# Feed-forward first layers on TensorE: one 512-column product over both parts of h, halves added afterwards, and the PSUM pools exchanged

## The chip, the cores and the metric

The kernel runs on one core of one Trainium2 chip. The metric is the device time of one execution in microseconds (us). Lower is better. The engines are called PE (TensorE, matrix products; PEld is its weight load), DVE (VectorE), ACT (ScalarE), POOL (GpSimd) and SP (SyncE, whose queue issues most of the transfers).

## The reference

Two transformer blocks over 256 tokens with 1024 features, in float32. The first holds a stick-breaking attention and a mixture of 32 experts and isn't touched by the change in what it computes. The second is cut here to what matters:

```python
def swiglu(x, w_in, w_out):
    gate, up = jnp.split(x @ w_in, 2, axis=-1)
    return (jax.nn.silu(gate) * up) @ w_out

x = x + 0.5 * swiglu(rmsnorm(x, ffn1_norm_g), ffn1_w_in, ffn1_w_out)
...
x = x + mixer(rmsnorm(x, mix_norm_g))
x = x + 0.5 * swiglu(rmsnorm(x, ffn2_norm_g), ffn2_w_in, ffn2_w_out)
x = rmsnorm(x, final_norm_g)
```

The hidden width of a feed-forward is 2816. The mixer runs an mLSTM branch and a gated unit (SGU) beside it, multiplies both by sigmoid gates, adds them and sends the sum through an output matrix.

## The kernel before, in words

**Numbers in two parts.** In the second block every float32 value that goes to PE is split into a rounded part r and a remainder l, and a product is taken as wr·hr + wr·hl + wl·hr. Weights are split as they arrive: `split_w` (L162) lets ACT copy 128x1024 values into r (L167) and DVE subtract to get l (L169). There are three buffers for each part, so a split waits until the matmuls of the third split before it are through.

**The feed-forward.** `ffn` (L774) is called twice: first layer and output of the first feed-forward carry the prefix fa, of the second fb. The hidden width is worked in NF = 22 tiles of 128. For tile j, `inner(j)` takes the product of the gate half and of the up half (i = 0, 1) with the whole h, over KT = 8 slices of 128 features, 256 tokens wide: `mm_feat` issues three matmuls of 256 columns for every slice. Both halves go into one PSUM bank, tile `gu`. `gated(j)` multiplies the bank by the normalisation factors `rb` (DVE, L787, from PSUM into SBUF), takes silu on ACT (L789), multiplies (L790) and splits the result into pr (L793) and pl (L794). `outer(j)` adds the tile's share of the second layer into accumulators in PSUM: for fa 8 blocks of 256 columns with three matmuls each, for fb 4 blocks of 512 columns. Up to three `inner` products run ahead of `gated` and `outer`. Names in the profile drop numbers at the end: `fagu` stands for all fagu0 to fagu21, `fawi20r` keeps its own.

**Head of a feed-forward.** The normalisation factor isn't known when the first products start. The squares of x are summed into rows, two matmul groups of one column (`fas` in fa, `fbs` in fb) sum them over the features, a chain of small DVE operations makes the inverse square root, and `spread` multiplies diagonal tiles with ones into `fab`/`fbb` and copies that to `rb` (L183). Only then can `gated(0)` run. The dictionary `between` puts these steps behind certain `inner` calls (1 and 2.5), and in fb it puts transposes of x (`tokens`, tiles x5t, copied by ACT, L1185) behind inner 5 to 8.

**The mixer.** Its projections are made by `tok_half`, 48 matmuls of 512 columns into one two-bank tile each (mv, mo, mg, ms and others). `gate` reads such a tile with a sigmoid on ACT (L1136) and multiplies on DVE (L1137). For the last pair (`ms`, halves 0 and 1) the loop goes on: DVE adds hm (L1149), PE transposes the sum in four pieces per block of tokens tb into tile `mT` (L1152), ACT and DVE split it into mr and ml. Then the output product `mo` accumulates with `mm_block`.

**PSUM.** There are two pools: `zt` gives one of 2 tiles of two banks, `gt` one of 4 tiles of one bank. A tile asked for when all are in use waits for the last reader of the oldest. Before the change the accumulators (fa, mo, fb) are the two `zt` tiles, and gu, fas, fab, fax, mT, x5t and the like share the four `gt` tiles.

**Order.** The order of instructions on each engine is made by the tile scheduler when the program is built; priorities (`high_priority` in `split_w`) and pins (`issue_after`) steer it. Each engine runs its list in order. The weights come through SP's queue.

Of the kernel before, what the change touches and what calls it, by code (L numbers as in the profile page):

```python
# [9 lines left out]
F32 = mybir.dt.float32  # L10
# [10 lines left out]
P = 128  # L21
# [20 lines left out]
def tile_model(ctx: ExitStack, tc: tile.TileContext, a, out, dbg=None):  # L42
# [135 lines left out]
    def spread(r, name):  # L178

        t = gt(name + "b", (P, T))  # L180
        for tb in range(2):
            mm(t[:, tb * P:(tb + 1) * P], ones, diag(r[:, tb:tb + 1], f"{name}d{tb}"), True, True)
        V.tensor_copy(rb, t)  # L183

    def h_tiles(name):
        return (hsp.tile([P, KT, T], F32R, tag="hr", name=name + "r"),
                hsp.tile([P, KT, T], F32R, tag="hl", name=name + "l"))

# [44 lines left out]
    A2 = cp.tile([P, KT], F32, name="A2")  # L233
    h1r, h1l = h_tiles("h1")

# [171 lines left out]
    for n_ in range(15):  # L407
        k, i = divmod(n_, 2)
        if n_ in (7, 8):
            w = hsp.tile([P, 2048], F32, tag=("hr", "hl")[n_ - 7], name=f"gu0{k}{i}")  # L410
            nc.sync.dma_start(w, a["moe_gu"][0, k, i])
        else:
            w = load(a["moe_gu"][0, k, i], f"gu0{k}{i}")
        ahead["gu", k, i] = [w[:, 512 * e:512 * e + 512] for e in range(4)]
        if n_ == 13:
            xn = hold("xn", (P, 2, D))
# [248 lines left out]
    def overflow():  # L665

        nv = nc.values_load(nover[0:1, 0:1], engines=LOOP_ENGINES, min_val=0, max_val=1)
        with tc.If(nv > 0):
            V.tensor_copy(pos[:, :, 0:1], pos[:, :, 0:1])
            hT = hsp.tile([P, KT, T], F32, tag="hr", name="ov_h")  # L670
            ya = [t4(f"ov_ya{tb}") for tb in range(2)]
# [7 lines left out]
            for qe in range(32):  # L679
                q, e = divmod(qe, 4)  # L680
                y = [zt(f"ov_y{qe}{tb}") for tb in range(2)]
                for f in range(4):
                    c0 = 512 * e + P * f
                    w = hsp.tile([P, 2, KT, P], F32, tag="hl", name=f"ov_w{qe}{f}")
                    for i in range(2):
# [31 lines left out]
    def new_h(name):  # L717
        hr, hl = h_tiles(name)
        return hr, hl, [None]

    def add_h(h, kt, gain):
        hr, hl, _ = h
        i = S.activation(hr[:, kt, :], xT[:, kt, :], AF.Identity, scale=gain[:, kt:kt + 1])
        return i, V.scalar_tensor_tensor(hl[:, kt, :], xT[:, kt, :], gain[:, kt:kt + 1], hr[:, kt, :].bitcast(F32),
                                         ALU.mult, ALU.subtract)

    def add_sq(h, kt, name):

        s_ = t1(f"{name}q{kt}")
        S.activation(s_, xT[:, kt, :], AF.Square, scale=1.0 / 32)  # L730
        if kt == 0:
            h[2][0] = s_
        else:
            G.tensor_tensor(h[2][0], h[2][0], s_, ALU.add)

    def scales(h, name):

        t = gt(name + "s", (P, 2))
        for tb in range(2):
            mm(t[:, tb:tb + 1], h[2][0][:, tb * P:(tb + 1) * P], ones[:, 0:1], True, True)  # L740
        v = sm(name + "_v", (P, 2))
        V.tensor_scalar(v, t, RMS_EPS, None, ALU.add)
        r = cp.tile([P, 2], F32, name=name + "_r")
        V.tensor_copy(r, rsqrt(v, 2, name))
        return r


    def block(acc, kt):
        return acc[kt % 2][:, kt // 4, 256 * (kt // 2 % 2):256 * (kt // 2 % 2) + 256]

    def mm_block(acc, kt, xr, xl, w, start, stop):

        o, cs = block(acc, kt), slice(kt * P, (kt + 1) * P)

        if start and kt // 2 % 2:
            with tc.issue_after(begun[kt % 2].ins):
                mm(o, w[0][:, cs], xr, False, False, skip_group_check=True)
        else:
            begun[kt % 2] = mm(o, w[0][:, cs], xr, start, False, skip_group_check=True)
        mm(o, w[0][:, cs], xl, False, False, skip_group_check=True)  # L760
        mm(o, w[1][:, cs], xr, False, stop, skip_group_check=True)

    begun = [None, None]

    def ffn(h, win, wout, name, between, finish, tail, by_token=False, pins={}):

        hr, hl, _ = h
        acc = [zt(f"{name}acc{tb}") for tb in range(2)]

        def inner(j):  # L770
            w = w8(f"{name}wi{j}", (P, 2, KT, P))
            for i in range(2 if j == 0 else 1):
                c = slice(i, i + 1) if j == 0 else slice(0, 2)
                nc.sync.dma_start(w[:, c], win[j][:, c])  # L774
            ps = gt(f"{name}gu{j}", (P, 2, T))
            for i in range(2):

                pin = (None, diag.last) if (j, i) == (3, 0) else pins.get((j, i), (None, None))
                wr, wl = split_w(w[:, i], f"{name}wi{j}{i}", pins=pin)
                mm_feat(ps[:, i, :], wr, wl, hr, hl)  # L780
                if i == 0 and j + 0.5 in between:
                    between[j + 0.5]()
            return ps

        def gated(j, ps):
            gu = t4(f"{name}sc{j}", (P, 2, T))
            V.tensor_tensor(gu, ps, rb[:, None, :].to_broadcast([P, 2, T]), ALU.mult)  # L787
            g = t1(f"{name}h{j}")
# [10 lines left out]
        def outer(j, part):  # L799
# [5 lines left out]
            if by_token:  # L805
                tb, hf = divmod(part, 2)
                ts = slice(tb * P, (tb + 1) * P)
                return mm_tok(acc[hf][:, tb, :], pr[:, ts], pl[:, ts], w[0][:, half(hf)], w[1][:, half(hf)],
                              j == 0, j == NF - 1)
# [4 lines left out]
        ahead = []  # L814
        for j in range(NF):
            while len(ahead) < 3 and j + len(ahead) < NF:
                n = j + len(ahead)
                ahead.append(inner(n))
                if n in between:
                    between[n]()  # L820
            if 0 < j <= NF - tail:
                for part in parts:
                    outer(j - 1, part)
# [61 lines left out]
    def first_scales():  # L885
        t = gt("fas", (P, 2, 2))
        for i in range(2):
# [10 lines left out]
    def first_x():  # L898

        nc.sync.dma_start(pk[:, PK_CW:PK_N], a["pk"][:, PK_CW:PK_N])  # L900
        r = rab
        t = gt("fax", (P, T))
        for tb in range(2):
            mm(t[:, tb * P:(tb + 1) * P], ones, diag(r[:, tb:tb + 1], f"faxd{tb}"), True, True)
        for kt in range(KT):
# [16 lines left out]

    hr, hl, _ = hm_

# [221 lines left out]
    for hf, tb in gate(10, zu, "ms"):  # L1146
        cs = slice(hf * 512, (hf + 1) * 512)
        ks = slice(4 * hf, 4 * hf + 4)
        V.tensor_tensor(zu[:, tb, cs], zu[:, tb, cs], hm[:, tb, cs], ALU.add)  # L1149
        t = gt(f"mT{hf}{tb}", (P, 4, P))  # L1150
        for kk in range(4):
# [49 lines left out]
    def last(acc, part):  # L1201
# [107 lines left out]
```

## Time and profile before

| what | value |
|---|---|
| runs | 1250.47, 1253.34, 1254.34 us; median 1253.34 |
| profiled execution | 1253.52 us, its span 1251.7 us |
| PE busy | 1091.1 us (87% of the span), 7409 instructions recorded |
| DVE, ACT, POOL busy | 596.9 us (48%), 448.1 us (36%), 35.0 us (3%) |
| granted TensorE clock, mean | 0.937 of full speed |
| chain that ended last | PE 47%, DMA 17%, DVE 2%, ACT 1% |

How to read it: 1.8 us of the execution lie outside the span. The experts of the first block are bound by transfers (the DMA terms of the chain), all before about 626 us. The second block runs from about 628 us to the end, with PE busy in nine tenths or more of most slices. "Granted clock" is the share of full TensorE speed (2.4 GHz) that the chip allowed; 0.50 is the lower level, 1.2 GHz. In a row of the trace, "x48" counts instructions, and "[1.66 <-PE ms L94]" says how long the engine was idle before the row and what ended it.

### The profile page before, as it was taken

To read this page: it belongs to the slowest core of one execution; us is meant where nothing else is said; L and a number is where in the kernel's file an instruction comes from. 1 tells how busy PE (TensorE), PEld (TensorE's weight loads), DVE (VectorE), ACT (ScalarE), POOL (GpSimd) and SP (SyncE) were. 2 spreads that over 40 slices of the span, in tenths; PEclk is the share of its full clock that TensorE was granted. 3 is DMA by queue.
4 is the path that set the end of the run, shared out by engine and by line. 5 is a ranking of instruction groups with operands and counts; after the bars stand their busy time and mean duration, and the time that the engine had idled before them with its cause. 6 is when DMAs were issued, how large, how long until landed. Compare 5 with 4: busy or idle time off the path is not lost.

```text
span 1251.7 us, 17974 instructions
## 1 busy us (share of the span) xinstructions
PE 1091.1 (87%) x7409; PEld 811.9 (65%) x7409; DVE 596.9 (48%) x1009; ACT 448.1 (36%) x654; POOL 35.0 (3%) x52
## 2 busy tenths in 40 slices
PE   5989998975776776676799999999999999999996
PEld 2778972321212231222289999988998889999995
DVE  5896441210101010110277555577879566755555
ACT  3465521100000000000254444457564455544443
POOL 0000000000000000000020000020000002000001
PEclk9998978988877788978899999999999999999999
DMA  9997679999999999999998430454446656464000
GB/s 387 420 364 312 220 279 420 423 423 423 424 424 420 424 424 423 423 423 424 421 423 345 172 135 1 161 193 165 172 151 269 236 203 251 169 234 174 30 1 34
DMA packets 51497, 357.39 MB, mean 286 GB/s; under 512 B 5840, under 2 KB 6096, under 8 KB 9552
## 3 DMA queue, kind: packets, MB, share of 16 engines
q1 hardware_dynamic: 50544, 353.54, 70.7%
q0 software_dynamic: 576, 2.10, 0.5%
q8 instruction: 60, 0.98, 0.3%
q10 hardware_dynamic: 288, 0.52, 0.1%
q14 instruction: 29, 0.24, 0.1%
HBM read 355.09 MB, written 1.05 MB: 285 GB/s over the span
## 4 chain that ended last, share of the span: by engine, by line
PE 47%; DMA 17%; DVE 2%; ACT 1%; issue 0%; POOL 0%; SPq 0%; DVEq 0%; ACTq 0%
DMA gu<-moe_gu 11%; PE fbgu L94 10%; PE fagu L94 9%; DMA d<-moe_d 6%; PE faacc L94 5%; PE fbacc L94 4%; PE mqk L94 4%; PE mo L94 3%; PE mv L94 2%; PE mz L94 2%; PE mu L94 2%; PE ms L94 2%; PE mg L94 2%; PE sc L94 0%; PE nu L94 0%
## 5 line engine op out<-in xcount | busy, mean ns | idle before, releaser
L94 PE MATMUL gu<-gu,xg 128*32 128x512 f32 x1024 | 147.4, 671 | 62.6 <-DMA gu<-moe_gu 62.5
L94 PEld LDWEIGHTS gu<-gu,xg 128*32 128x32 f32 x1024 | 24.8, 113 | 134.7 <-DMA gu<-moe_gu 77.3
L94 PE MATMUL Y<-d,HT 128*32 128x512 f32 (+1 forms) x544 | 83.8, 725 | 25.8 <-DMA d<-moe_d 19.9
L596 DVE TENSOR_SCALAR xg<-xgp,A,mod 128x128 f32<-128x128 f32 x32 | 13.1, 410 | 174.5 <-PE xgp L94 174.5
L661 DVE SCALAR_TENSOR_TENSOR xT<-cmb,g,xT 128x256 f32<-128x256 f32 x60 | 27.8, 484 | 127.0 <-PE cmb L94 126.7
L594 ACT ACTIVATE xg<-xgp,mod,A 128x128 f32<-128x128 f32 x32 | 14.7, 458 | 173.0 <-PE xgp L94 173.0
L94 PEld LDWEIGHTS xgp<-eq,xn 128*128 128x128 f32 x256 | 40.0, 225 | 55.0 <-issue 53.3
L94 PEld LDWEIGHTS Y<-d,HT 128*32 128x32 f32 x544 | 15.8, 128 | 78.2 <-DMA d<-moe_d 47.8
L94 PE MATMUL xgp<-eq,xn 128*128 128x128 f32 x256 | 50.2, 333 | 7.9 <-DVE eq L584 7.0
L655 ACT ACTIVATE Ys<-Y 128x512 f32<-128x512 f32 x15 | 9.0, 597 | 121.3 <-PE Y L94 121.3
L94 PE MATMUL cmb<-CT,Ys 128*128 128x256 f32 x128 | 41.0, 451 | 11.3 <-ACT Ys L655 10.3
L94 PEld LDWEIGHTS cmb<-CT,Ys 128*128 128x128 f32 x128 | 25.0, 218 | 37.5 <-ACT Ys L655 25.5
L617 DVE TENSOR_TENSOR H<-H,gu 128x512 f32<-128x512 f32 x8 | 5.5, 688 | 64.2 <-ACT H L616 64.2
L616 ACT ACTIVATE H<-gu 128x512 f32<-128x512 f32 x8 | 4.8, 597 | 57.5 <-PE gu L94 57.5
L854 POOL TENSOR_TENSOR faq<-faq,faq 128x256 f32<-128x256 f32 x10 | 10.1, 1035 | 459.1 <-ACT faq L850 458.9
L975 DVE SCALAR_TENSOR_TENSOR cv<-cs,pk,cv 128x255 f32<-128x255 f32 (+2 forms) x48 | 22.3, 478 | 0.4
L620 PEld LDWEIGHTS HTp<-kc,H 128*128 128x128 f32 x32 | 4.9, 189 | 25.1 <-DVE H L617 25.1
L787 DVE TENSOR_TENSOR fbsc<-fbgu,rb 128x512 f32<-128x512 f32 x22 | 15.0, 690 | 10.9 <-PE fbgu L94 10.8
L787 DVE TENSOR_TENSOR fasc<-fagu,rb 128x512 f32<-128x512 f32 x22 | 15.0, 691 | 10.5 <-PE fagu L94 10.5
L278 DVE SCALAR_TENSOR_TENSOR crow<-adar,crow 128x1024 f32<-128x1024 f32 x16 | 19.5, 1218 | 0.1
L620 PE MATMUL HTp<-kc,H 128*128 128x128 f32 x32 | 7.7, 386 | 13.1 <-DVE H L617 13.1
L614 ACT ACTIVATE CT<-ctp 128x256 f32<-128x256 f32 x8 | 3.1, 385 | 31.6 <-PE ctp L612 31.6
(2253 smaller groups left out, 3521.1 us busy)
## 6 DMA issues: line engine op xcount, KB each, us to landing
gu<-moe_gu SPq DMA_DIRECT2D x127, 1024.0 KB, 19.7
d<-moe_d SPq DMA_DIRECT2D x60, 1024.0 KB, 19.7
fawi<-f1i SPq DMA_DIRECT2D x21, 1024.0 KB, 17.3
fbwi<-f2i SPq DMA_DIRECT2D x21, 1024.0 KB, 4.8
ada<-ada SPq DMA_DIRECT2D x16, 1024.0 KB, 10.0
fawo<-f1o SPq DMA_DIRECT2D x11, 1024.0 KB, 15.7
fbwo<-f2o SPq DMA_DIRECT2D x11, 1024.0 KB, 4.8
wqk<-sbqk SPq DMA_DIRECT2D x8, 1024.0 KB, 11.7
```

The source lines that it names most:

```text
L94: return PE.matmul(o, l, r, start=start, stop=stop, **kw)
L278: V.scalar_tensor_tensor(c[:, 1], w[:, D * j:D * j + D], 1.0, c[:, 0], ALU.mult, ALU.mult, accum_out=mod[:, 1, j, kt:kt + 1])
L594: S.activation(xg[:, k, :], t, AF.Identity, scale=A2[:, k:k + 1], bias=sh2[:, k:k + 1])
L596: V.tensor_scalar(xg[:, k, :], t, A2[:, k:k + 1], sh2[:, k:k + 1], ALU.mult, ALU.add)
L616: S.activation(H, gu[:, 0, :], AF.Silu)
L617: V.tensor_tensor(H, H, gu[:, 1, :], ALU.mult)
L620: PE.transpose(ht[:, f, :], H[:, f * P:(f + 1) * P], ident)
L655: S.activation(Ys, Y, AF.Copy)
L661: V.scalar_tensor_tensor(xT[:, kt, :], c[:, kk, :], g2[:, kt:kt + 1], xT[:, kt, :], ALU.mult, ALU.add)
L787: V.tensor_tensor(gu, ps, rb[:, None, :].to_broadcast([P, 2, T]), ALU.mult)
L854: (V if i and kt > 3 else G).tensor_tensor(sums[i], sums[i], s_, ALU.add)
L975: V.scalar_tensor_tensor(cv[:, d:T], ts[:, 0:T - d], pk[:, cw + 3 - d:cw + 4 - d], cv[:, d:T], ALU.mult, ALU.add)
```

## The change

`h_tiles` makes one tile in which the r and the l part of a slice stand side by side, so that a matmul can stream both as 512 columns. `mm_pair` replaces `mm_feat` in `inner`: for each slice one matmul wr·[hr | hl] of 512 columns into a bank, and one wl·hr of 256 columns into its first half (in the last slice the order of the two is turned). The tile `gu` has two banks now, one for gate, one for up, and comes from `zt`. Afterwards ACT copies both second halves to SBUF (L794 of the changed kernel) and DVE adds the first halves (L795); `gated` multiplies by `rb` in SBUF (L799).

The pools are exchanged with it: the accumulators are four `gt` tiles, and fas/fbs, fab/fbb, fax, mT and x5t, which were `gt` tiles, are `zt` tiles, of which there are two. mT holds both blocks of tokens of a half in one tile. fax is copied to SBUF by ACT. The loop over j is written as one over n, with the same order of calls (inner n, outer n-3, gated n-2). A load of the first block (gu02) and its overflow branch take other buffers of the same size.

```diff
     def spread(r, name):
-        t = gt(name + "b", (P, T))
+        t = zt(name + "b")[:, 0, 0:T]
...
     def h_tiles(name):
-        return (hsp.tile([P, KT, T], F32R, tag="hr", name=name + "r"),
-                hsp.tile([P, KT, T], F32R, tag="hl", name=name + "l"))
+        hp = hsp.tile([P, KT, 2, T], F32R, tag="h", name=name)
+        return hp[:, :, 0, :], hp[:, :, 1, :], hp
...
+    def mm_pair(o, wr, wl, hp):
+
+        for k in range(KT):
+            for i in (1, 0) if k == KT - 1 else (0, 1):
+                if i == 0:
+                    mm(o, wr[:, k, :], hp[:, k].rearrange("p i t -> p (i t)"), k == 0, k == KT - 1, skip_group_check=True)
+                else:
+                    mm(o[:, 0:T], wl[:, k, :], hp[:, k, 0, :], False, False, skip_group_check=True)
...
     def scales(h, name):
-        t = gt(name + "s", (P, 2))
+        t = zt(name + "s")[:, 0, 0:2]
...
     def block(acc, kt):
-        return acc[kt % 2][:, kt // 4, 256 * (kt // 2 % 2):256 * (kt // 2 % 2) + 256]
+        return acc[kt % 4][:, T * (kt // 4):T * (kt // 4) + T]
...
-        acc = [zt(f"{name}acc{tb}") for tb in range(2)]
+        acc = [gt(f"{name}acc{b}") for b in range(4)]
...
-            ps = gt(f"{name}gu{j}", (P, 2, T))
+            ps = zt(f"{name}gu{j}")
...
-                mm_feat(ps[:, i, :], wr, wl, hr, hl)
+                mm_pair(ps[:, i, :], wr, wl, h[2])
                 if i == 0 and j + 0.5 in between:
                     between[j + 0.5]()
-            return ps
-
-        def gated(j, ps):
             gu = t4(f"{name}sc{j}", (P, 2, T))
-            V.tensor_tensor(gu, ps, rb[:, None, :].to_broadcast([P, 2, T]), ALU.mult)
+            S.activation(gu, ps[:, :, T:2 * T], AF.Copy)
+            V.tensor_tensor(gu, gu, ps[:, :, 0:T], ALU.add)
+            return gu
+
+        def gated(j, gu):
+            V.tensor_tensor(gu, gu, rb[:, None, :].to_broadcast([P, 2, T]), ALU.mult)
...
     def first_scales():
-        t = gt("fas", (P, 2, 2))
+        t = zt("fas")[:, 0, 0:4].rearrange("p (i b) -> p i b", i=2)
...
-        t = gt("fax", (P, T))
+        ps = zt("fax")[:, 0, 0:T]
...
+        t = t1("faxs")
+        S.activation(t, ps, AF.Copy)
...
-        t = gt(f"mT{hf}{tb}", (P, 4, P))
+        if tb == 0:
+            mT = zt(f"mT{hf}")
+        t = mT[:, tb, :].rearrange("p (k t) -> p k t", k=4)
...
-    acc = [zt(f"mo{tb}") for tb in range(2)]
+    acc = [gt(f"mo{b}") for b in range(4)]
...
     def tokens(tb, hf):
-        t = gt(f"x5t{tb}{hf}", (P, 4, P))
+        t = zt(f"x5t{tb}{hf}")[:, 0, :].rearrange("p (k t) -> p k t", k=4)
```

Three places show how the lists of the engines move. The first is PE's list inside the first layer of tile 15 of fa (fagu). Here far and fal are the r and l part of h, fa is the tile that holds both, and fawi150r/l are the split gate weights. Before:

```order
L94 MATMUL fagu_9198<-far,fawi150r 128x256
L94 MATMUL fagu_9198<-fal,fawi150r 128x256
L94 MATMUL fagu_9198<-far,fawi150l 128x256
L94 MATMUL fagu_9198<-far,fawi150r 128x256
L94 MATMUL fagu_9198<-fal,fawi150r 128x256
L94 MATMUL fagu_9198<-far,fawi150l 128x256
```

and of the change:

```order
L94 MATMUL fagu_8862<-fa,fawi150r 128x512
L94 MATMUL fagu_8862<-fa,fawi150l 128x256
L94 MATMUL fagu_8862<-fa,fawi150r 128x512
L94 MATMUL fagu_8862<-fa,fawi150l 128x256
```

Two slices take four matmuls in place of six. Over both feed-forwards PE's list is 704 matmuls shorter (2 x 22 tiles x 2 halves x 8 slices).

The second is PE's list where the first half of ms ends (ms with 011r), the second begins (100r), and the transposes mT follow. Before, the transposes come behind 37 matmuls of the second half, of which the first rows stand here, and both blocks of tokens together:

```order
L94 MATMUL ms_11707<-ms011r,mxr 128x512
L94 MATMUL ms_11707<-ms011l,mxr 128x512
L94 MATMUL ms_11707<-ms011r,mxl 128x512
L94 MATMUL ms_11798<-ms100r,mxr 128x512
L94 MATMUL ms_11798<-ms100l,mxr 128x512
...
L1152 MATMUL mT_11780<-kc,zu 128x128 x4
L1152 MATMUL mT_11791<-kc,zu 128x128 x4
```

and of the change (h of the mixer is mx here):

```order
L94 MATMUL ms_11271<-ms011l,mx 128x512
L94 MATMUL ms_11271<-ms011r,mx 128x512
L1170 MATMUL mT_11344<-kc,zu 128x128 x4
L94 MATMUL ms_11361<-ms100r,mx 128x512
L94 MATMUL ms_11361<-ms100l,mx 128x512
...
L1170 MATMUL mT_11344<-kc,zu 128x128 x4
```

The first four transposes now stand directly behind the first half of ms and ahead of all of the second, the other four behind 22 matmuls of it. The second half of ms takes the PSUM tile of the first, mT the other one.

The third is ACT's list around tile 5 of fb: fbwi51r and fbwi60r are the r parts of weights (up half of tile 5, gate half of tile 6), x<-x5t the copy of transposed x. Before:

```order
L167 ACTIVATE fbwi51r<-fbwi_12567 128x1024
L789 ACTIVATE fbh_12742<-fbsc_12740 128x256
L1185 ACTIVATE x_12151<-x5t_12626 128x512
L793 ACTIVATE fbpr_12745<-fbh_12742 128x256
L167 ACTIVATE fbwo2r<-fbwo_12556 128x1024
L167 ACTIVATE fbwi60r<-fbwi_12657 128x1024
```

and of the change:

```order
L167 ACTIVATE fbwo2r<-fbwo_12054 128x1024
L801 ACTIVATE fbh_12211<-fbsc_12035 128x256
L805 ACTIVATE fbpr_12214<-fbh_12211 128x256
L794 ACTIVATE fbsc_12107<-fbgu_12066 128x512
L1203 ACTIVATE x_11714<-x5t_12110 128x512
L801 ACTIVATE fbh_12287<-fbsc_12107 128x256
L805 ACTIVATE fbpr_12290<-fbh_12287 128x256
L167 ACTIVATE fbwi60r<-fbwi_12140 128x1024
```

The split of the next weights, fbwi60r, now stands behind the new copy of tile 5 (fbsc<-fbgu), the copy of x5t, and the silu and pr of tile 5.

SP's list is the same in both, and so is all of PE's list ahead of fa.

## Rows read from the trace of the kernel before

**Rows 1.** Windows of fa, fb: length; PE, PEld, DVE, ACT, POOL busy; PEclk; DMA share, GB/s.

```profile
728.40:806.20 77.80, 77.80 (x651) 77.80 (x650) 45.39 (x55) 34.20 (x46) 0.59 (x6) 1.00 0.25 89
1131.10:1225.00 93.90, 93.90 (x666) 88.50 (x665) 55.44 (x66) 42.05 (x56) 0.00 (x0) 1.00 0.19 68
```

**Rows 2.** Chain that ended last, one round of fa: start, us, what.

```profile
728.41 5.76 PE fagu L94 x48
734.17 2.88 PE faacc L94 x24
```

**Rows 3.** The same view, fb: the second layer's share of one round.

```profile
1128.36 2.75 PE fbacc L94 x12
```

**Rows 4.** The same view, head of fa.

```profile
639.63 2.89 PE fagu L94 x22
642.52 0.79 PE fas L94 x8
643.31 5.62 PE fagu L94 x46
648.93 0.46 PE fab L94 x4
649.41 0.43 DVE rb L183
649.98 6.23 PE fagu L94 x50
```

**Rows 5.** Timeline of DVE, head of fa: start, us, instruction.

```profile
640.90 1.22 DVE L169 TENSOR_TENSOR fawi20l<-fawi,fawi20r 128x1024 fp32r<-128x1024 f32 x1
...
643.54 0.16 DVE L894 SCALAR_TENSOR_TENSOR v<-v,fas 128x2 f32<-128x2 f32 x1
```

**Rows 6.** Costliest groups: 128x512 operations that read PSUM, on ACT and DVE.

```profile
L655 ACT ACTIVATE Ys<-Y 128x512 f32<-128x512 f32 x15 | 9.0, 597 | 121.3 <-PE Y L94 121.3
L787 DVE TENSOR_TENSOR fasc<-fagu,rb 128x512 f32<-128x512 f32 x22 | 15.0, 691 | 10.5 <-PE fagu L94 10.5
```

**Rows 7.** Timelines of PE, ACT and DVE where the first half of ms ends.

```profile
1012.88 0.39 PE L94 MATMUL ms<-ms011r,mxl 128*128 128x512 f32 x1
1013.11 0.39 PE L94 MATMUL ms<-ms100r,mxr 128*128 128x512 f32 x1
...
1013.30 1.06 ACT L167 ACTIVATE ms110r<-ms 128x1024 fp32r<-128x1024 f32 x1 [1.66 <-PE ms L94]
1014.27 1.25 ACT L1136 ACTIVATE mss<-ms,mx_r 128x512 f32<-128x512 f32 x2
...
1015.54 1.29 DVE L1137 TENSOR_TENSOR zu<-zu,mss 128x512 f32<-128x512 f32 x2
1016.75 1.29 DVE L1149 TENSOR_TENSOR zu<-zu,hm 128x512 f32<-128x512 f32 x2
```

**Rows 8.** Windows: stretches in which PE waited, each with the one behind it.

```profile
90.90:93.70 2.80, 0.00 (x0) 0.00 (x0) 1.90 (x3) 1.68 (x3) 0.00 (x0) 0.82 1.01 421
93.70:99.50 5.80, 5.77 (x25) 5.77 (x26) 4.24 (x7) 4.02 (x5) 0.00 (x0) 0.50 0.99 420
116.90:118.30 1.40, 0.00 (x0) 0.00 (x0) 0.54 (x1) 0.83 (x2) 0.00 (x0) 1.00 1.05 445
120.00:123.40 3.40, 3.40 (x18) 3.40 (x17) 1.30 (x3) 2.15 (x3) 0.00 (x0) 0.50 0.93 393
629.10:630.40 1.30, 0.00 (x0) 0.00 (x0) 1.30 (x3) 1.30 (x3) 0.00 (x0) 1.00 1.03 435
630.50:640.00 9.50, 9.25 (x75) 9.05 (x76) 7.23 (x8) 8.60 (x17) 8.53 (x8) 1.00 1.02 423
```

**Rows 9.** Timeline of ACT, round 5 of fb: silu, copy of x5t, split of fbwi60.

```profile
1084.98 0.40 ACT L789 ACTIVATE fbh<-fbsc 128x256 f32<-128x256 f32 x1
1085.28 0.58 ACT L1185 ACTIVATE x<-x5t 128x512 f32<-128x512 f32 x1
1090.13 1.06 ACT L167 ACTIVATE fbwi60r<-fbwi 128x1024 fp32r<-128x1024 f32 x1 [1.50 <-PE fbgu L94]
```

More of the change, by code (lines that the diff above doesn't have):

```diff
@@ L233, in tile_model @@
     A2 = cp.tile([P, KT], F32, name="A2")
-    h1r, h1l = h_tiles("h1")
+    h1r, h1l, _ = h_tiles("h1")
     def mod_mm(u, name):
@@ L409, in tile_model @@
         if n_ in (7, 8):
-            w = hsp.tile([P, 2048], F32, tag=("hr", "hl")[n_ - 7], name=f"gu0{k}{i}")
+            if n_ == 7:
+                gu2 = hsp.tile([P, 2, 2048], F32, tag="h", name="gu02")
+            w = gu2[:, n_ - 7]
             nc.sync.dma_start(w, a["moe_gu"][0, k, i])
@@ L669, in overflow @@
             V.tensor_copy(pos[:, :, 0:1], pos[:, :, 0:1])
-            hT = hsp.tile([P, KT, T], F32, tag="hr", name="ov_h")
+            ov = hsp.tile([P, 2, 2048], F32, tag="h", name="ov")
+            hT = ov[:, 0].rearrange("p (k t) -> p k t", k=KT)
+            w = ov[:, 1].rearrange("p (i k c) -> p i k c", i=2, k=KT)
             ya = [t4(f"ov_ya{tb}") for tb in range(2)]
@@ L683, in overflow @@
                     c0 = 512 * e + P * f
-                    w = hsp.tile([P, 2, KT, P], F32, tag="hl", name=f"ov_w{qe}{f}")
                     for i in range(2):
@@ L717, in new_h @@
     def new_h(name):
-        hr, hl = h_tiles(name)
-        return hr, hl, [None]
+        return *h_tiles(name), [None]
     def add_h(h, kt, gain):
-        hr, hl, _ = h
+        hr, hl = h[:2]
         i = S.activation(hr[:, kt, :], xT[:, kt, :], AF.Identity, scale=gain[:, kt:kt + 1])
@@ L731, in add_sq @@
         if kt == 0:
-            h[2][0] = s_
+            h[3][0] = s_
         else:
-            G.tensor_tensor(h[2][0], h[2][0], s_, ALU.add)
+            G.tensor_tensor(h[3][0], h[3][0], s_, ALU.add)
     def scales(h, name):
-        t = gt(name + "s", (P, 2))
+        t = zt(name + "s")[:, 0, 0:2]
         for tb in range(2):
-            mm(t[:, tb:tb + 1], h[2][0][:, tb * P:(tb + 1) * P], ones[:, 0:1], True, True)
+            mm(t[:, tb:tb + 1], h[3][0][:, tb * P:(tb + 1) * P], ones[:, 0:1], True, True)
         v = sm(name + "_v", (P, 2))
@@ L748, in block @@
     def block(acc, kt):
-        return acc[kt % 2][:, kt // 4, 256 * (kt // 2 % 2):256 * (kt // 2 % 2) + 256]
+        return acc[kt % 4][:, T * (kt // 4):T * (kt // 4) + T]
     def mm_block(acc, kt, xr, xl, w, start, stop):
         o, cs = block(acc, kt), slice(kt * P, (kt + 1) * P)
-        if start and kt // 2 % 2:
-            with tc.issue_after(begun[kt % 2].ins):
+        if start and kt // 4:
+            with tc.issue_after(begun[kt % 4].ins):
                 mm(o, w[0][:, cs], xr, False, False, skip_group_check=True)
         else:
-            begun[kt % 2] = mm(o, w[0][:, cs], xr, start, False, skip_group_check=True)
+            begun[kt % 4] = mm(o, w[0][:, cs], xr, start, False, skip_group_check=True)
         mm(o, w[0][:, cs], xl, False, False, skip_group_check=True)
         mm(o, w[1][:, cs], xr, False, stop, skip_group_check=True)
-    begun = [None, None]
+    begun = [None] * 4
     def ffn(h, win, wout, name, between, finish, tail, by_token=False, pins={}):
-        hr, hl, _ = h
-        acc = [zt(f"{name}acc{tb}") for tb in range(2)]
+        acc = [gt(f"{name}acc{b}") for b in range(4)]
         def inner(j):
@@ L807, in outer @@
                 ts = slice(tb * P, (tb + 1) * P)
-                return mm_tok(acc[hf][:, tb, :], pr[:, ts], pl[:, ts], w[0][:, half(hf)], w[1][:, half(hf)],
+                return mm_tok(acc[part], pr[:, ts], pl[:, ts], w[0][:, half(hf)], w[1][:, half(hf)],
                               j == 0, j == NF - 1)
@@ L814, in ffn @@
         ahead = []
-        for j in range(NF):
-            while len(ahead) < 3 and j + len(ahead) < NF:
-                n = j + len(ahead)
+        for n in range(NF + 2):
+            if n < NF:
                 ahead.append(inner(n))
@@ L820, in ffn @@
                     between[n]()
+            j = n - 2
+            if j < 0:
+                continue
             if 0 < j <= NF - tail:
@@ L901, in first_x @@
         r = rab
-        t = gt("fax", (P, T))
+        ps = zt("fax")[:, 0, 0:T]
         for tb in range(2):
-            mm(t[:, tb * P:(tb + 1) * P], ones, diag(r[:, tb:tb + 1], f"faxd{tb}"), True, True)
+            mm(ps[:, tb * P:(tb + 1) * P], ones, diag(r[:, tb:tb + 1], f"faxd{tb}"), True, True)
+        t = t1("faxs")
+        S.activation(t, ps, AF.Copy)
         for kt in range(KT):
@@ L920, in tile_model @@
         return
-    hr, hl, _ = hm_
+    hr, hl = hm_[:2]
     def tok_half(i, name):
@@ L1206, in last @@
         xs = x[:, tb, half(hf)]
-        V.scalar_tensor_tensor(xs, acc[hf][:, tb, :], 0.5, xs, ALU.mult, ALU.add)
+        V.scalar_tensor_tensor(xs, acc[part], 0.5, xs, ALU.mult, ALU.add)
         sq(xs, ss[:, 0, hf:hf + 1], f"fin{tb}{hf}")
```

## The prediction

> **What bounds the kernel now.** I first read the windows for two steady stretches of the second block. In both PE is busy all the time, 77.80 of 77.80 us in fa and 93.90 of 93.90 us in fb, at a granted clock of 1.00, while DVE works 45.39 and 55.44 us and ACT 34.20 and 42.05 us, and the transfers take a quarter of the DMA engines or less [rows 1]. So there only a shorter list for PE makes a round shorter. Then the chain of waits: a round of fa is 5.76 us of first layer (48 matmuls) and 2.88 us of second layer (24 matmuls), 120 ns for every matmul of 256 columns [rows 2]. In fb the second layer takes 2.75 us for 12 matmuls of 512 columns, 229 ns each [rows 3]. Last I read the places between such stretches where PE waits for a few DVE and ACT operations in turn: the head of a feed-forward [rows 4, 5] and the end of the first half of ms [rows 7]. They matter because the changed lists put a wait on PE there. PE has no slack around them, so what it waits is paid in full.
>
> **The change part by part**, against the profiled execution of 1253.52 us, which stands 0.18 us above the median of the runs, 1253.34 us.
>
> *First layers.* A slice took 3 x 120 = 360 ns, and will take one matmul of 512 and one of 256 columns, 229 + 120 = 349 ns [rows 2, 3]: 11 ns less. A round has 16 slices, so it gains 0.173 us. I count 19 rounds of each feed-forward, 3 to 21, since rounds 0 to 2 belong to the heads below: 38 x 0.173 = 6.6 us less. The bounds are nothing (the columns are the same, 768 a slice) and 14.6 us (24 ns a slice, the third rival below). I take 11 ns since both durations come from stretches without waits.
>
> The rows themselves say what a matmul costs beyond its columns: 256 columns at 2.4 GHz are 106.7 ns, 512 are 213.3 ns, so 13.3 and 15.8 ns are left over [rows 2, 3]. The Trainium skill ("TensorE: Matmul & The Clock Gate", section Back-to-back issue gap) speaks against the change here: it gives a single matmul N/2.4 + 2.5 ns at full clock, so that one matmul fewer would save only 2.5 ns and the first layers only 38 x 16 x 2.5 ns = 1.5 us by my estimate from that page. The trace doesn't agree with it in this stream, where a weight load stands between any two matmuls; the rows decide, and the smaller gain stays as a rival.
>
> *What is added to ACT and DVE in a round.* One copy of 128x512 on ACT, 0.60 us by the copy Ys<-Y, and one add of 128x512 on DVE, 0.69 us by fasc<-fagu,rb [rows 6]. A round of 8.64 us holds 45.39/77.80 of DVE work, 5.0 us, and 3.8 us of ACT work [rows 1]; 5.7 and 4.4 us still fit under 8.5 us. A gu tile has now 2 buffers for 4, so the products of tile n+2 wait for the add of tile n; between them stand the products of tile n+1 and a second layer, some 8 us, against 0.60 + 0.69 us. Cost nothing. Were that cover gone, it would be up to 1.3 us a round.
>
> *Head of fa.* Before, PE went from the second half of fagu1 (released at 639.63) to fas at 642.52 and to fagu2 at 643.31, and fagu3 began at 649.98, when the copy rb was done [rows 4]. Now fas takes a tile that fagu0 held, so it waits for the new add of tile 0, which stands on DVE behind fawi20l (640.90 + 1.22 = 642.12): 642.8 us [rows 5, 6]. fas takes 0.79 us [rows 4], the two operations v read it behind the next split, which moves by the 0.69 us of the add to about 643.9, and fagu2, which takes the tile of fas, starts behind the second v at about 644.3: 1.0 us late [rows 5]. fagu2 takes 16 x 0.349 = 5.58 us, fab 0.46, the copy rb 0.43, and fagu3, which takes the tile of fab, starts at 650.95: still 1.0 us late. Behind it, the split of fawi30 and the second layer's weights are as early as before. Cost +1.0 us (0 to 2).
>
> *Head of fb.* The same steps in the same order on the same engines; +1.0 us by the same rows (0 to 2).
>
> *ACT in round 5 of fb.* fbwi60r stands now behind the copy of tile 5, the copy of x5t, silu and pr of tile 5. All of these wait for the end of fbgu5: copy 0.60, add 0.69, times rb 0.69 [rows 6], silu 0.40, multiply and pr about 0.4 each, so with the passes between engines about 3.4 us, then the split's 1.06 us [rows 9]. PE has the second layer, 2.75 us [rows 3], and four transposes, some 0.4 us, until it needs fbwi60r: it waits 1.4 us, and another 0.7 us at once for fbwi60l behind it. Before, the split ran without any of this [rows 9]. Cost +2.1 us (0 if the products of fbgu6 find other work, 3 if the passes are slow).
>
> *The end of the first half of ms.* Before, ms of the second half started at 1013.11, right behind the last matmul of the first half, in the free PSUM tile [rows 7]. Now that tile is mT's, and the four transposes of the first block of tokens stand first in PE's list. They wait for zu<-zu,hm, and that for zu<-zu,mss, for mss on ACT, and for ms110r ahead of it on ACT. All four keep their order, so the first add ends where it did, at 1016.75 + 0.69 = 1017.4 [rows 7]. Even without the transposes the second half of ms would wait for the two mss, which read its tile until 1015.5. PE, which then has ms and mo without a break ahead of it, starts 4.3 us later. The weights of ms wait for these matmuls in turn, and nothing behind gives time back. Cost +4.3 us (4.0 to 4.6).
>
> *The clock after that.* The trace shows what a gap on PE can do: 2.8 us without a matmul were followed by 5.8 us at a granted clock of 0.50, 1.4 us in another place by 3.4 us at 0.50, 1.3 us at the start of fa by none [rows 8]. A stretch of matmuls at 1.2 GHz loses half its length: 1.7 to 2.9 us. I take 2.3 us (0 to 2.9). The other gaps that I expect, 0.3 to 1.4 us, are nearer to the one that cost nothing; I put nothing in for them.
>
> *The rest.* fax's copy on ACT, the four accumulators, the loads of the first block: off the path, since the order there is the same and SP's queue has not moved. Nothing.
>
> Sum: -6.6 + 1.0 + 1.0 + 2.1 + 4.3 + 2.3 = +4.1 us, 1257.6 us, or 1257.4 us seen from the median.
>
> **The rivals.** About 0.3% (3.8 us) is what a measurement of this kernel can tell from no change: 1249.6 to 1257.1 us.
>
> 1. *The clock holds through the gap in ms* (the other side: not slower). For it: at the start of fa PE stood 1.3 us and the clock stayed at 1.00; the mixer, too, has been full of matmuls for long. Against: this gap is three times as long, and the 2.8 us gap was followed by 0.50 [rows 8]. Its price is the term of 2.3 us: 1255.1 us, within 0.3%. It decides in the windows behind 1017 us.
>
> 2. *The clock also falls elsewhere*, behind the 1.4 + 0.7 us in fb or in a head. For it: the 1.4 us gap with 3.4 us at half behind it [rows 8]. Each such fall loses 1.7 us: 1259.1 us for one, 1260.8 us for two.
>
> 3. *Weight loads set the 120 ns.* In fa, PEld is busy 77.80 of 77.80 us [rows 1]. If a matmul of 256 columns takes 120 ns only because its load must finish, the load for wl hides under the 512 columns, and a slice takes 229 + 107 = 336 ns, 13 ns less than in the sum: 38 x 16 x 13.3 ns = 8.1 us, 1249.3 us. Against: with 512 columns, where a load has twice the time, 15.8 ns are still left over. A rule of the Trainium skill ("Trainium Kernel Development and Optimization", section Best Practices) bids to judge PE by the busy share of its weight loads rather than of its matmuls; by it this rival would be the likely one, and the row of 512 columns is why I hold it for unlikely.
>
> 4. *A matmul fewer saves next to nothing*, because the leftover goes with the columns or because the second product writes the bank that the first has just left. With nothing saved the sum loses its 6.6 us: 1264.0 us. Against: 120 and 229 ns are both means over long rows without a wait [rows 2, 3]. By the 2.5 ns that the Trainium skill gives (the page and section named above) it would be 1262.5 us, an estimate.
>
> **How the numbers follow.** Forecast 0.48, rival 1 0.25, rival 2 0.15, rival 3 0.07, rival 4 0.05. The forecast's own range is 1255.5 to 1259.5 us (the heads and the fb wait by their bounds). The range of 8 in 10, 1251.0 to 1261.5 us, takes in rivals 1 and 2 and leaves 3 and 4 out; its low end is rival 1 with the heads and the fb wait at half. Faster than 1249.6 us: rival 3, and a little for a sum in which most waits find cover, 0.10. Within 0.3%: rival 1 and the lower part of the forecast, 0.42. Slower: 0.48.
>
> **What would show it.** Right: in a steady round of fa 32 first-layer matmuls in about 5.6 us; PE idle for 4.3 us behind the first half of ms, ended by DVE zu<-zu,hm, and 0.50 in the clock behind it; an idle of about 1.4 us ahead of fbgu6, ended by ACT fbwi60r; fagu3 some 1.0 us later than before. Wrong: a round of 5.4 us (rival 3) or 5.75 us (rival 4); a clock of 1.00 behind ms (rival 1); or 0.50 in fa or fb (rival 2). What would overthrow the whole is waits in every steady round, on the new copy or the add.

## The result, and the profile after

The changed kernel takes 1260.07 us (median of 7 runs, 1257.87 to 1262.59), the kernel before 1251.94 us (7 runs by then, 1250.47 to 1256.13). The ratio is 1.0062 with a 95% interval of 1.0050 to 1.0075: slower by some 8 us. (This ratio and those below are taken over all runs and are not quotients of the two medians.) The forecast was 1257.4 us, range 1251.0 to 1261.5. Direction and mechanism came out, the size was about half.

The first lines of the page after, with the columns of the table before:

```profile
span 1256.5 us, 16680 instructions
PE 1073.4 (85%) x6705; PEld 769.6 (61%) x6705; DVE 625.0 (50%) x1053; ACT 469.5 (37%) x699; POOL 34.4 (3%) x52
```

PE works 17.7 us less than before over the whole span, but most of that lies in the first block. Between the first matmul of fa and the last of fb PE is busy for 607.4 us against 608.0 before, and idle for 13.9 us against 5.1. So the kernel is longer because PE waits more; the shorter list hardly shows in the busy time, in part because the clock fell twice in this stretch, of which more below.

The first block ended 3.4 us earlier in this profile than in that of before. The change gives other buffers of the same size to one load of it and to its overflow branch and nothing more, the block is bound by transfers, and the medians don't show a difference. So all that follows is counted from the first matmul of fa on: from there to the last matmul of fb it is 8.16 us longer, against 8.13 us in the medians. That the two agree so closely is partly chance, since the profiled execution of the changed kernel took 1258.32 us, 1.75 us less than its median.

The chain in the stretch that answers to [rows 2] (start, us, what):

```profile
725.10 5.60 PE fagu L94 x32
730.70 2.88 PE faacc L94 x24
733.58 5.60 PE fagu L94 x32
```

A first layer takes 5.60 us for 32 matmuls in place of 5.76 for 48: 350 ns a slice. And the waits of PE in the second block, longest first (engine, line, waited for: us in total, times, longest):

```profile
PE mT L1170 <- DVE zu L1165: 4.2, 1, 4.2
PE fagu L94 <- DVE fawi00l L169: 1.4, 1, 1.4
PE fbgu L94 <- ACT fbwi60r L167: 1.3, 1, 1.3
...
PE fbacc L94 <- ACT fbpr L805: 0.5, 1, 0.5
PE fbgu L94 <- DVE fb_v L753: 0.5, 1, 0.5
PE fagu L94 <- DVE v L908: 0.5, 1, 0.5
PE fbgu L94 <- DVE rb L183: 0.5, 1, 0.5
PE fagu L94 <- DVE rb L183: 0.5, 1, 0.5
...
PE fas L94 <- DVE fasc L795: 0.4, 1, 0.4
PE fbgu L94 <- DVE fbwi60l L169: 0.3, 1, 0.3
```

The longest one stands where the prediction put it; the second, for fawi00l, was there before the change with the same 1.4 us. The chain at the longest shows each link of it, and what comes after:

```profile
1009.91 1.06 ACT ms110r L167
1010.97 0.02 issue
1011.00 1.23 DVE ms110l L169
1012.22 1.20 DVE zu L1153 x2
1013.42 0.61 DVE zu L1165
1014.04 0.04 issue
1014.08 0.66 PE mT L1170 x4
1014.74 6.64 PE ms L94 x22
```

From the last matmul of the first half (ended about 1009.9) to 1014.08 PE stands for 4.2 us. Then 22 matmuls take 6.64 us, 302 ns each, where 229 ns are usual [rows 3]. The windows say why (length; PE, PEld, DVE, ACT, POOL busy; granted clock; DMA share, GB/s):

```profile
1010.00:1013.90 3.90, 0.00 (x0) 0.00 (x0) 2.90 (x4) 2.12 (x3) 0.00 (x0) 1.00 0.81 298
1014.00:1015.90 1.90, 1.82 (x9) 1.55 (x10) 0.99 (x3) 0.60 (x1) 0.00 (x0) 0.77 0.00 0
1016.00:1017.70 1.70, 1.70 (x6) 1.33 (x5) 0.23 (x1) 0.00 (x0) 0.00 (x0) 0.50 0.00 0
1019.00:1021.00 2.00, 2.00 (x11) 1.62 (x10) 0.80 (x1) 1.06 (x1) 0.00 (x0) 1.00 0.00 0
```

The clock falls to 0.50, the lower level, behind the gap, as behind the first two gaps of [rows 8], and is back before 1019 us. (The kernels below that keep a gap of 4.2 us here, unfilled, show such a fall behind it too.)

The starts of the same instructions in both traces, subtracted, give the whole account of the 8.16 us. The column "expected" has the terms of the prediction, the 6.6 us of the rounds in two halves:

| stretch, between first matmuls | expected | found |
|---|---|---|
| head of fa, up to fagu3 | +1.0 | +1.27 |
| rounds of fa, fagu3 to fagu21, and the end of fa | -3.3 | -2.79 |
| mixer, in the middle | 0 | +1.48 |
| first half of ms to the first matmul of mo | +4.3 and +2.3 | +6.09 |
| mo | 0 | +0.57 |
| head of fb, up to fbgu3 | +1.0 | +1.53 |
| the wait for fbwi60r and fbwi60l | +2.1 | +1.60 |
| rounds of fb and the end | -3.3 | -1.59 |
| sum | +4.1 | +8.16 |

### The profile page after: what moved, and what is told of

Read it like the earlier page. It is cut to its first block, busy times and chain, and to the rows that moved or that the text cites. A ratio compares the mean times of both kernels' runs of the same rounds, so it can differ in the third digit from the quotient of the medians.

```text
span 1256.5 us, 16680 instructions
## 1 busy us (share of the span) xinstructions
PE 1073.4 (85%) x6705; PEld 769.6 (61%) x6705; DVE 625.0 (50%) x1053; ACT 469.5 (37%) x699; POOL 34.4 (3%) x52
## 4 chain that ended last, share of the span: by engine, by line
PE 59%; DMA 32%; DVE 5%; ACT 2%; issue 1%; SPq 0%; POOL 0%; ACTq 0%; DVEq 0%
DMA gu<-moe_gu 20%; DMA d<-moe_d 11%; PE fbgu L94 10%; PE fagu L94 9%; PE faacc L94 5%; PE fbacc L94 4%; PE qk L94 4%; PE mqk L94 4%; PE mo L94 3%; PE y L94 2%; PE ms L94 2%; PE mz L94 2%; PE mu L94 2%; PE mg L94 2%; PE v L94 2%; PE mv L94 2%
## 5 line engine op out<-in xcount | busy, mean ns | idle before, releaser
L94 PE MATMUL gu<-gu,xg 128*32 128x512 f32 x1024 | 141.5, 646 | 73.6 <-DMA gu<-moe_gu 73.5
L94 PE MATMUL Y<-d,HT 128*32 128x512 f32 (+1 forms) x544 | 80.2, 698 | 26.8 <-DMA d<-moe_d 20.8
L795 DVE TENSOR_TENSOR fbsc<-fbsc,fbgu 128x512 f32<-128x512 f32 x22 | 15.0, 681 | 2.7 <-ACT fbsc L794 2.7
L799 DVE TENSOR_TENSOR fbsc<-fbsc,rb 128x512 f32<-128x512 f32 x22 | 15.1, 690 | 0.6
L799 DVE TENSOR_TENSOR fasc<-fasc,rb 128x512 f32<-128x512 f32 x22 | 15.1, 691 | 0.6
```

The source lines that it names most:

```text
L94: return PE.matmul(o, l, r, start=start, stop=stop, **kw)
L795: V.tensor_tensor(gu, gu, ps[:, :, 0:T], ALU.add)
L799: V.tensor_tensor(gu, gu, rb[:, None, :].to_broadcast([P, 2, T]), ALU.mult)
```

## The experiments

The theory after this reading (A): the pair of matmuls gives what the rows say, and the loss is waits that the exchange of the pools puts on PE, each by itself. The rival (B): PE is short of PSUM tiles now, and a wait taken away in one place comes back in the next. All kernels below start from the changed one; the runs of the kernel before had medians of 1251.2 to 1251.7 us beside them.

**All of mT in one-bank tiles.**

```diff
-        if tb == 0:
-            mT = zt(f"mT{hf}")
-        t = mT[:, tb, :].rearrange("p (k t) -> p k t", k=4)
+        t = gt(f"mT{hf}{tb}", (P, 4, P))
```

> The changed kernel with one edit: the four transposed pieces mT are one-bank tiles (gt) again, as before the change. Theory A (the loss comes from waits that the exchange of the PSUM pools puts on PE, each where it shows): the second half of ms starts right behind the first again, the 4.2 us gap and the half clock behind it go, and the way from the first ms matmul to the first mo matmul is 22.7 us as before and not 28.8 us: about 6 us less, near 1254 us. Theory B (PE pays for the exchange wherever it is next short of banks): the four accumulators of mo, which now share the four banks with mT, wait for the reads of mT, and 3 us or more of the 6 come back there: 1257 us or more.

1260.39 us, ratio to the kernel before 1.0075 (1.0059 to 1.0092): nothing gained. B was right here, and more than it said: all of it came back. The timeline of PE has the same wait, only later, at the second half (start, us, instruction, idle before it and what ended it):

```profile
1026.10 1.12 PE L1168 MATMUL mT<-kc,zu 128*128 128x128 f32 x4 [4.21 <-DVE zu L1165]
```

In the changed kernel the first ms stands for 4.2 us and mo fills PE while mT of the second half waits; here the first is free, but mT has taken the banks that mo's accumulators want, mo can't start, and the second gap is open. (That the banks are what holds mo is shown by the next kernel.) The kernel before had both covered: ms1 in its own tile, mo in another.

**mT of half 0 in one-bank tiles, of half 1 in a two-bank tile.** This gives ms1 its own tile and mo its four banks:

```diff
-        if tb == 0:
-            mT = zt(f"mT{hf}")
-        t = mT[:, tb, :].rearrange("p (k t) -> p k t", k=4)
+        if hf == 0:
+            t = gt(f"mT0{tb}", (P, 4, P))
+        else:
+            if tb == 0:
+                mT = zt("mT1")
+            t = mT[:, tb, :].rearrange("p (k t) -> p k t", k=4)
```

> The changed kernel with one edit: mT of half 0 takes two one-bank tiles, mT of half 1 stays one two-bank tile. In the kernel with all mT in one-bank tiles the gap only moved to the end of ms, because mo's four accumulators then had to wait for banks and could not fill PE while mT of half 1 waited. Theory A (each of the two gaps is a shortage of PSUM tiles of one kind at one moment): now ms of half 1 has a free two-bank tile and mo has four banks ahead of mT of half 1, no gap of over 1 us stands between the first ms and the mo matmuls, and the way from the first ms to the first mo matmul is 22.7 us or a little more: 5.5 to 6.5 us less than the changed kernel, near 1254 us. Rival: the transposes need their zu whatever the tiles are, and a gap of some 4 us turns up in a third place: 1258 to 1260 us.

1253.86 us, ratio 1.0017 (1.0008 to 1.0027): 6.2 us less than the changed kernel. The chain has no wait there any more:

```profile
1004.78 13.61 PE ms L94 x60
1018.39 0.87 PE mT L1173 x8
1019.26 2.54 PE ms L94 x11
1021.80 6.84 PE mo L94 x58
```

From the first ms to the first mo it is 22.69 us; the kernel before took 22.69, the changed one 28.77, the one with all mT in one-bank tiles 28.68. Theory A with the correction that the place has two waits and both have to be covered.

**The gap filled with matmuls.** 18 matmuls that nobody reads are issued behind the first half of ms:

```diff
+        if (hf, tb) == (0, 0):
+            fill = gt("fill")
+            for i in range(18):
+                with tc.issue_after(tok_half.last.ins):
+                    mm(fill, hr[:, 0, 0:P], hm_[2][:, 0].rearrange("p i t -> p (i t)"), True, True)
```

> The changed kernel with 18 matmuls of 512 columns added, which only fill PE's gap behind the first half of ms (they write a free bank that nobody reads; 18 x 0.229 = 4.1 us of a 4.2 us gap). Theory A: the granted clock stays at 1.00 there, the 22 ms matmuls behind take 5.0 us and not 6.6, and the way from the gap to mo is 1.5 to 2 us shorter; the gap itself stays. Total 1258 us. Rival: the clock falls there whatever PE does, or the ms matmuls are slow for another reason (a wait on a weight split): no change, 1260 us.

1256.94 us, ratio 1.0054 (1.0037 to 1.0070). The windows of this kernel:

```profile
1010.00:1013.90 3.90, 3.79 (x17) 2.81 (x15) 3.06 (x5) 1.96 (x3) 0.00 (x0) 1.00 0.85 284
1014.00:1021.00 7.00, 7.00 (x35) 5.89 (x36) 2.39 (x3) 2.56 (x3) 0.00 (x0) 1.00 0.04 7
```

mT starts as late as in the changed kernel, but the clock stays at 1.00 and the way from ms to mo is 27.18 us, 1.6 us shorter. So of the 6.09 us there, 1.6 are the clock and 4.5 the wait. The medians gained 3.1 us, and this trace doesn't account for the other half: from the first matmul of fa to the last of fb it is 1.74 us shorter than that of the changed kernel. It lacks the dip of the clock in the mixer, 1.5 us, of which more below, but has one of the same price in the head of fa, where the granted clock is 0.51 from 642.2 to 645.7 us.

**x5t later.**

```diff
-        between[5 + i] = lambda i=i: tokens(*divmod(i, 2))
+        between[10 + i] = lambda i=i: tokens(*divmod(i, 2))
```

> The changed kernel with one edit: the transposes of x (x5t) follow the first layers of tiles 10 to 13 of fb and not of tiles 5 to 8. Theory A: fbwi60r no longer stands behind the copy of x5t, silu and pr of tile 5, so the wait of 1.4 + 1.1 us that the trace shows ahead of fbgu6 goes: about 2 us less, near 1258 us. Theory B: the wait is made by the new copy and the add in a crowded round, and turns up in round 10 or 11: no change, 1260 us.

1259.64 us, ratio 1.0066 (1.0049 to 1.0083): no gain. (The two waits for fbwi60r and fbwi60l that were expected to go are 1.26 and 0.33 us; the 1.1 us of the expectation belong to fbwi10l, in the head of fb.) The wait ahead of fbgu6 is gone and stands ahead of fbgu11, the round behind the first x5t, with the same length:

```profile
1145.25 0.51 PE L94 MATMUL fbgu<-fb,fbwi110r 128*128 128x512 f32 x1 [1.26 <-ACT fbwi110r L167]
1146.51 0.39 PE L94 MATMUL fbgu<-fb,fbwi110l 128*128 128x256 f32 x1 [0.32 <-DVE fbwi110l L169]
```

B again, in that the wait came back, though by another reason than B gave: the rounds ahead of round 10, with the same copy and add, run at 8.36 us each without a wait, and what moved is the first x5t. An x5t in a gu tile changes ACT's order wherever it is put. In this trace the clock fell behind the wait as well (0.89 on the mean from 1145 to 1160 us), which in that of the changed kernel it didn't.

**The heads.** The accumulators are asked for only behind the head, so its tiles can have their banks for that time:

```diff
-        t = zt(name + "b")[:, 0, 0:T]
+        t = gt(name + "b", (P, T))
...
-        t = zt(name + "s")[:, 0, 0:2]
+        t = gt(name + "s", (P, 2))
...
-        acc = [gt(f"{name}acc{b}") for b in range(4)]
+        acc = []
...
+            if not acc:
+                acc.extend(gt(f"{name}acc{b}") for b in range(4))
...
-        t = zt("fas")[:, 0, 0:4].rearrange("p (i b) -> p i b", i=2)
+        t = gt("fas", (P, 2, 2))
```

> The changed kernel with the heads undone: fas, fbs, fab, fbb are one-bank tiles again, and the accumulators of both feed-forwards are asked for behind them. Theory A: fas no longer waits for the add of tile 0, nor fagu2 for the two v, nor fagu3 for the copy rb; from the first fagu1 matmul with wi11 to the first of fagu3 it is 11.0 us or less and not 12.5, and the same in fb: about 2.5 us less, near 1257.5 us. Theory B: the heads are bound by the chain of small DVE operations, with the add of tiles 0 and 1 now among them: 0.5 us less at most.

1253.84 us, ratio 1.0026 (1.0015 to 1.0037): 6.2 us less than the changed kernel, more than twice what was expected. The chain of the head of fa has none of the three waits:

```profile
635.65 2.83 PE fagu L94 x15
638.48 0.79 PE fas L94 x8
639.26 5.91 PE fagu L94 x33
645.17 0.45 PE fab L94 x4
645.62 5.61 PE fagu L94 x32
```

fas follows the products of tile 1, the products of tile 2 follow fas, and those of tile 3 no longer wait for the copy rb. From the first matmul with fawi11 to the first of fagu4 it is 16.03 us, against 18.22 in the changed kernel and 16.83 in the one before; from the first mo matmul with mwo7 to fbgu4 29.36 us against 31.18 and 29.68. That is 2.2 + 1.8 = 4.0 us; 1.5 us more are the dip in the mixer, which this profile doesn't have. Whether the runs behind the medians differ by that dip isn't shown, so the heads are worth 4.0 us and not 6.2. What was expected was short because the free tiles take away a wait (for rb) that the kernel before had too.

**The pools alone.** The first layers as three matmuls again:

```diff
-                mm_pair(ps[:, i, :], wr, wl, h[2])
+                mm_feat(ps[:, i, 0:T], wr, wl, h[0], h[1])
...
-            S.activation(gu, ps[:, :, T:2 * T], AF.Copy)
-            V.tensor_tensor(gu, gu, ps[:, :, 0:T], ALU.add)
+            S.activation(gu, ps[:, :, 0:T], AF.Copy)
```

> The changed kernel with the first layers as three matmuls of 256 columns a slice again; the pools stay exchanged and ACT's copy stays (of the whole product, so the add is not there). Theory A (the pair saves 0.15 us a round and the exchange costs what the waits cost): a steady round takes 8.64 us and not 8.49, the waits in ms and the half clock stay, the heads are 0.5 us shorter each without the add: 1262 to 1264 us. Rival (the pair saves nothing over a whole kernel): 1259 to 1260 us.

1260.48 us, ratio 1.0073 (1.0057 to 1.0088), hardly above the changed kernel, as the rival had it. The trace says otherwise for the rounds themselves:

```profile
726.40 5.76 PE fagu L94 x48
732.16 2.88 PE faacc L94 x24
```

They are 5.76 us again. From fagu3 to fagu21 this kernel takes 2.5 us more than the changed one, from fbgu3 to the end 1.9 us more. But its heads are 1.1 and 1.0 us shorter, since no add stands in DVE's list ahead of fas and fbs, and it has no dip in the mixer, 1.5 us. The two cancel the gain: a comparison of totals would have called the pair worthless.

**All mended.** The free accumulators of the heads, mT of half 0 and 1 in different tiles, and the transposes x5t in one-bank tiles in the head of fb, ahead of the accumulators:

```diff
-        t = zt(f"x5t{tb}{hf}")[:, 0, :].rearrange("p (k t) -> p k t", k=4)
+        t = gt(f"x5t{tb}{hf}", (P, 4, P))
...
-    between = {1: last_scales, 2.5: lambda: spread(rfb[0], "fb")}
-    for i in range(4):
-        between[5 + i] = lambda i=i: tokens(*divmod(i, 2))
+    between = {0: lambda: (tokens(0, 0), tokens(0, 1)), 1: last_scales, 2.5: lambda: spread(rfb[0], "fb"),
+               2: lambda: (tokens(1, 0), tokens(1, 1))}
```

> The pair of 512 and 256 columns with the waits taken away: fas, fbs, fab, fbb and the transposes of x5t use one-bank tiles ahead of the accumulators, which are asked for behind them (x5t so moves to the head of fb), mT of half 0 in one-bank tiles and of half 1 in a two-bank tile. Theory A: ms 6 us, the heads 4.6 us and fbgu6 2 us less than the changed kernel, which leaves the gain of the rounds: 1260 - 12.5 = 1247.5 us, 3 to 4 us less than the kernel before. Rival: x5t in the head of fb makes that head longer by its four copies of 0.58 us on ACT and its 16 transposes: 1250 us, no faster than before.

1244.05 us, ratio 0.9946 (0.9933 to 0.9960): 7.6 us less than the kernel before, 16 us less than the changed one, better than expected. By the traces it is 15.0 us less: 6.1 from ms to mo, 3.8 in the two heads, 3.5 in rounds 4 to 9 of fb, where the waits and the transposes are gone, and 1.5 for the dip in the mixer, which nothing in the edit was meant to remove. The longest waits of PE in the second block are:

```profile
PE fagu L94 <- DVE fawi00l L169: 1.4, 1, 1.4
PE mv L94 <- DVE mv001l L169: 0.9, 1, 0.9
PE mo L94 <- DVE xT L1194: 0.6, 1, 0.6
PE fbacc L94 <- ACT fbpr L805: 0.5, 1, 0.5
```

The first was there before the change (1.4 us too), and the second stands at the head of the mixer, where PE waited 1.0 us for mxl before. None ahead of fbgu6 is left: with x5t out of the gu tiles the order of ACT in the rounds is regular. So B is no rule: with the same two pools, of the waits that the exchange brought only the 0.5 us for fbpr at the end of fb is left on this list.

**All mended, without the pair.** The edit of the pools-alone kernel, made in the mended one.

> The mended kernel (the one with the waits taken away) with the first layers as three matmuls of 256 columns a slice again, the rest as it is; ACT's copy stays, the add is not there. It measures the pair by itself where no wait is in its way. Theory A: 0.15 us a round over about 36 rounds: 5 to 6 us slower than the mended kernel, 1249 to 1250 us, and still 1.5 to 2.5 us faster than the kernel before because of its heads. Rival (most of the mended kernel's gain comes from the heads and the moved x5t, and the pair brings little, as the pools-alone run would have it): at most 2 us slower, 1246 us.

1250.07 us, ratio 0.9992 (0.9982 to 1.0001): like the kernel before. So where no wait is in its way, the pair is worth 6.0 us (1250.07 - 1244.05), by the traces 5.5 us from the first matmul of fa to the last of fb. (The add on DVE goes with the pair, so this is the value of both together.)

## Why the prediction was right in direction and short in size

*The rounds.* Predicted 38 x 0.173 = 6.6 us. A steady round of fa gives 0.155 us (8.64 - 8.49), since a slice takes 350 ns and not 349, one of fb 0.14 us (8.50 - 8.36), and in the changed kernel the stretches of the rounds got 4.4 us together (-2.79 and -1.59 in the table). This term was mis-sized by 2.2 us. Some 1.0 us of it is the smaller gain of the steady rounds. Half a microsecond more is lost in fb, in the round behind the wait for fbwi60r and behind fbgu21, where PE now waits 0.5 us for fbpr; the rest is spread over rounds that aren't steady. In the mended pair of kernels, 6.0 us are the value of the pair, near the 6.6. Rival 3 (weight loads set the 120 ns) falls: 5.4 us a round would have shown it. Rival 4 falls as well. The issue gap of 2.5 ns that the Trainium skill ("TensorE: Matmul & The Clock Gate", section Back-to-back issue gap) gives for an isolated matmul, by which the pair would be worth 1.5 us by estimate, doesn't fit the 6.0 us measured here, in a stream of weight loads and matmuls.

*The head of fa* was +1.0, found +1.27; *the head of fb* +1.0, found +1.53. The steps are those named. In fa these are fas behind the new add, fagu2 behind v, and fagu3 behind the copy rb, each with its own wait in the list above (that for rb was 0.4 us before); in fb the list has the last two of them. The head of fb was not worked out from its own rows but set equal to that of fa, and that missed 0.5 us.

*The wait for fbwi60r* was 1.4 + 0.7 us, found 1.26 + 0.33 us idle and 1.60 us in all, behind the chain that was foretold. The chain of the changed kernel:

```profile
1097.09 0.61 ACT fbsc L794
...
1097.72 0.70 DVE fbsc L795
...
1098.45 0.71 DVE fbsc L799
...
1099.17 0.43 ACT fbh L801
...
1099.62 0.44 DVE fbh L802
...
1100.08 0.42 ACT fbpr L805
1100.50 0.96 ACT fbwi60r L167
```

Copy, add, times rb, silu, multiply, pr, split: 0.61, 0.70, 0.71, 0.43, 0.44, 0.42 and about 1 us, as taken from [rows 6, 9]. What was too large is the second wait, 0.33 us for 0.7: the transposes of x5t, which the prediction put ahead of fbwi60r, stand between the first matmul of fbwi60r and that of fbwi60l, and fill part of it. The x5t later shows that it isn't tied to round 6.

*The end of ms.* +4.3 us for the wait and +2.3 us for the clock; found 4.5 and 1.6 us, told apart by the filled gap. The price of the clock had been taken in the middle between 1.7 and 2.9 us; the fall seen here cost about the lower one. What the prediction said of the mechanism holds, but it named one gap where the tiles make two: it said "nothing behind gives time back", and didn't see that mo's free banks cover the second one. The kernel with all mT in one-bank tiles showed that.

*What the sum left out.* It had no term for +1.48 us in the mixer, where the instructions haven't moved, and none for the wait at the end of fb, nor for +0.57 us in mo. The last stands in the traces of all nine changed kernels (+0.45 to +0.95), and its cause wasn't looked for. The rounds, 2.2 us, and the dip in the mixer, 1.5 us, make up most of the missing 4 us. Rival 2 (the clock falls elsewhere too) had the right kind of event, at 1.5 us rather than 1.7. In the trace of the changed kernel it is in a place that rival 2 didn't name; in the traces of four other kernels it is where rival 2 had it, behind the wait in fb or in a head. How many of the runs behind the median have such a dip, and where, isn't shown.

*Range and luck.* The forecast's own range, 1255.5 to 1259.5 us, missed; only the wide one holds the 1260.07 us, at the place of rival 2 with two falls, while the trace has other terms there. That is luck. The low end of the wide range also has a slip: rival 1 with the heads and the fb wait at half is 1253.1 us, and 1251.0 us is rival 1 with all three at nothing.

Rival 1 (the clock holds) falls by the windows behind 1014 us.

## What to carry to other kernels

A change that saves work on the bound engine can lose by the buffers that it takes: list, for every tile that changes pools, who is the next to want that tile, and what must have read it. Look at both sides of a place before mending it: a wait taken from one user of a pool may only pass to the next one. Totals that agree can hide a gain and a loss of the same size. Compare the starts of the same instructions in two traces, stretch by stretch.

## What the runs showed of the hardware that was not expected

The clock can dip without a gap on PE that the records show. In four of ten profiles (the changed kernel, all mT in one-bank tiles, mT split, x5t later) the granted clock fell in the middle of the mixer, in a stretch where PE's instructions are the same in all ten and in which PE is busy throughout. The windows from 858 to 868 us, of the changed kernel and then of the one with the heads mended, which is 2.9 us further on in its list there:

```profile
858.00:868.00 10.00, 10.00 (x65) 9.03 (x65) 5.27 (x11) 9.48 (x18) 0.00 (x0) 0.83 0.29 106
```

```profile
858.00:868.00 10.00, 10.00 (x83) 9.71 (x82) 4.34 (x8) 9.89 (x19) 0.00 (x0) 1.00 0.32 116
```

From the first mqk to the first mg it is 144.87 to 144.92 us in the four and 143.39 to 143.43 us in the other six, so the dip costs 1.5 us. Ahead of it stand small matmuls (dm and gtr), in which PE is busy by its records. Why it comes in some programs and not in others wasn't settled; each trace is of one execution, and the stretch comes at a slightly different time in each. A loss of that kind is near the size of the terms here, so it has to be found in the windows before a total is explained.

The same uncertainty holds behind the wait for fbwi60r. The clock stayed at 1.00 there in the changed kernel, with 1.26 us of idle PE, and was 0.87 on the mean in the kernel with mT split, with the same idle, from 1094.2 to 1095.5 us:

```profile
1097.00:1110.00 13.00, 11.41 (x61) 9.29 (x60) 6.96 (x8) 6.93 (x10) 0.00 (x0) 1.00 0.38 149
```

```profile
1097.00:1110.00 13.00, 13.00 (x63) 11.12 (x63) 6.83 (x7) 4.95 (x7) 0.00 (x0) 0.87 0.55 204
```

From fbgu6 to fbgu7 this kernel took 1.5 us longer than the changed one, and so did the one with all mT in one-bank tiles, where the clock fell too:

```profile
1102.00:1110.00 8.00, 7.67 (x33) 6.41 (x34) 4.70 (x4) 3.38 (x4) 0.00 (x0) 0.79 0.59 213
```

Six of the traces have this wait of 1.25 us or more, ahead of fbgu6 or fbgu11. In three (mT split, all mT in one-bank tiles, x5t later) the clock fell behind it, in three (the changed kernel, the heads, the filled gap) it didn't. So a short wait has two prices, its own length or that and about 1.5 us.
